# Cutting the first load of a cosine-similarity kernel by partitions: 16 rows, then 112, both issued ahead of the opening barrier

## The chip, the cores and the metric

One core of one Trainium2 chip. The metric is the device time of one execution in microseconds (us); every run below is of state fast with a granted clock of 1.0, except the two benches, which ran once each (state unknown) and are only compared within themselves. "Span" is first to last instruction in the profile, 1.8 to 2.2 us less than the device time here.

## The reference, cut to what matters

```python
x, y: float32 [8192, 8192]
x_norm = np.linalg.norm(x, axis=1, keepdims=True)
y_norm = np.linalg.norm(y, axis=1, keepdims=True)
return np.sum(x * y, axis=1) / (x_norm.squeeze() * y_norm.squeeze() + 1e-8)
```

Both inputs, 537 MB, are read once; for each row three sums are needed.

## The kernel before

The rows come in groups of 256, two rows to a partition, so that one load is 128 partitions x 16384 floats: 64 KB per partition, 8 MiB in all. (Below, a "row" is what one partition takes from one load, 64 KB, and a "row time" is the 2.42 us that it usually needs.) Three slots hold loads, x and y by turns. ScalarE (ACT) squares and sums, VectorE (DVE) forms the dot products, PE's sequencer hands the landings on to both. The last 512 rows come in smaller pieces.

```python
def load(src, m):
    return nc.sync.dma_start(out=slots[m % SLOTS], in_=src).then_inc(landed[m % SLOTS], 16)
...
load(xg[0, 0], 0)
load(yg[0, 0], 1)
load(xg[0, 1], 2)

with nc.sync.Fori(0, R - 1) as r:
    for m in range(SLOTS, 3 * SLOTS):
        ...
        take(nc.sync, used)              # a slot is free again
        load(src[r + g // SLOTS, g % SLOTS], m)
...
with nc.tensor.Fori(0, R):
    for m in range(2 * SLOTS):
        take(nc.tensor, landed[m % SLOTS], 16)
        nc.tensor.sem_inc(for_act, 1)
        nc.tensor.sem_inc(for_dve, 1)
```

A function that runs when the program is finished moves the first DMA instruction ahead of the opening barrier:

```python
load = next(i for i in body.instructions if i.opcode == "DMACopy")
...
opening.instructions = head[:at] + [load] + head[at:]
```

## Time and profile before

| | before |
|---|---|
| device time, median | 1249.38 us (1249.23 to 1249.7, 3 runs) |
| span | 1247.6 us |
| ACT busy / DVE busy | 916.9 / 698.2 us |
| share of 16 DMA engines taken by the load queue | 99.6% |
| first ACTIVATE on data | 22.36 us |

The prediction shows the lines of the profile that carry this. One view more is needed later: what the DMA engines moved in each of 40 equal slices of 31 us, in GB/s, from the page of the kernel before.

```profile
GB/s 435 431 414 435 437 437 437 437 435 435 433 412 437 437 437 437 437 437 435 435 424 420 437 437 437 437 437 437 433 433 412 437 437 437 437 437 437 418 425 335
```

The stream is flat from the first slice to the last but one. The dips I read as the counting of whole 64 KB packets in a slice, for the packets' own times stay at 2.42 us throughout (108 of 7680 took over 2.44).

### The profile page before, as it was taken

Reading aid. Unit: us, or ns where it says so; the run is one execution under the profiler, and the core shown is the slowest. Engines: PE = TensorE matmul, PEld = TensorE weight load, DVE = VectorE, ACT = ScalarE, POOL = GpSimd, SP = SyncE. Lnnn points to the kernel's source line nnn. Section 1 sums busy time; section 2 is a strip of 40 time slices with the busy share of each in tenths; the row PEclk is TensorE's granted clock in tenths of the full one; section 3 lists DMA queues with packets and bytes.
Section 4 is the critical chain, followed back from the end, with each engine's and each line's share of the span. In section 5 each row is a group of like instructions: output and inputs, shape, how many; then the busy total and the mean of one; then the engine's idle time right before and its main releaser. Section 6 shows DMA issues by size and latency. Waiting matters only on the chain. (4 is left out here: it accounts for less than half of the span.)

```text
span 1247.6 us, 1785 instructions
## 1 busy us (share of the span) xinstructions
PE 1.3 (0%) x4; PEld 0.3 (0%) x4; DVE 698.2 (56%) x252; ACT 916.9 (73%) x285; POOL 0.8 (0%) x8
## 2 busy tenths in 40 slices
PE   0000000000000000000000000000000000000000
PEld 0000000000000000000000000000000000000000
DVE  1654576545765447654467544675446755457566
ACT  3686776867768668677686776867868668677888
POOL 0000000000000000000000000000000000000000
DMA  9999999999999999999999999999999999999998
GB/s 435 431 414 435 437 437 437 437 435 435 433 412 437 437 437 437 437 437 435 435 424 420 437 437 437 437 437 437 433 433 412 437 437 437 437 437 437 418 425 335
DMA packets 11575, 536.93 MB, mean 430 GB/s; under 512 B 1299, under 2 KB 1845, under 8 KB 2613
## 3 DMA queue, kind: packets, MB, share of 16 engines
q1 hardware_dynamic: 11528, 536.88, 99.6%
q10 hardware_dynamic: 45, 0.03, 0.0%
q14 instruction: 2, 0.02, 0.0%
HBM read 536.87 MB, written 0.03 MB: 430 GB/s over the span
## 5 line engine op out<-in xcount | busy, mean ns | idle before, releaser
L142 ACT ACTIVATE junk<-slot 128x8192 uint8<-128x8192 f32 (+4 forms) x138 | 900.8, 6528 | 326.2 <-ACTq L139 320.5
L145 DVE CUSTOM_DVE_ANT_0 slot<-slot,slot 128x4096 f32<-128x4096 f32 (+1 forms) x60 | 391.1, 6556 | 452.4 <-DVEq L139 452.4
L212 DVE COPY side<-slot 128x4096 f32<-128x4096 f32 x30 | 132.8, 4428 | 71.7 <-DVEq L139 71.7
L145 DVE CUSTOM_DVE_ANT_0 side<-side,slot,part 128x4096 f32<-128x4096 f32 x30 | 134.6, 4488 | 0.0
L145 DVE CUSTOM_DVE_ANT_0 slot<-slot 128x8192 f32<-128x8192 f32 (+3 forms) x5 | 29.6, 5944 | 20.4 <-ACT junk L142 12.7
L142 ACT ACTIVATION_READ_ACCUMULATOR junk<-slot (+1 forms) x138 | 25.7, 186 | 0.0
L145 DVE CUSTOM_DVE_ANT_0 vjunk<-slot 128x384 uint8<-128x384 f32 (+4 forms) x8 | 6.8, 886 | 1.0 <-DMA slot<-in_y_dram 1.0
L145 DVE DVE_READ_ACCUMULATOR2_ANT gsum<- x60 | 6.7, 112 | 0.0
L145 DVE DVE_READ_ACCUMULATOR2_ANT part<- 128x1 f32 x30 | 2.5, 83 | 0.0
L192 ACT ACT_TABLE_LOAD x1 | 1.3, 1283 | 1.0 <-SPq L168 1.0
L350 PE MATMUL side<-ident,gden 128*30 128x128 f32 x2 | 0.6, 395 | 1196.9 <-DVE gden L344 1196.9
L194 ACT ACT_TABLE_LOAD x1 | 1.3, 1283 | 0.1
L145 DVE DVE_READ_ACCUMULATOR2_ANT parts<- 128x1 f32 x11 | 0.9, 82 | 0.0
L353 DVE COPY orow<-side 30x128 f32<-30x128 f32 x2 | 0.5, 279 | 0.6 <-PE side L350 0.6
L371 ACT COPY dots<-side 4x128 f32<-4x128 f32 x1 | 0.3, 254 | 0.7 <-PE side L369 0.7
L145 DVE CUSTOM_DVE_ANT_0 vjunk<-slot,base 128x384 uint8<-128x384 f32 x1 | 0.6, 619 | 0.1
L381 DVE TENSOR_TENSOR orl<-side,dots 4x128 f32<-4x128 f32 x1 | 0.3, 279 | 0.5 <-PE side L379 0.5
L270 DVE RECIPROCAL gden<-gden 128x60 f32<-128x60 f32 x1 | 0.5, 529 | 0.0
L350 PEld LDWEIGHTS side<-ident,gden 128*30 128x30 f32 x2 | 0.1, 107 | 1196.8 <-issue 1196.8
L369 PE MATMUL side<-ident,bsum 128*4 128x128 f32 x1 | 0.4, 373 | 46.9 <-DVE bsum L145 46.9
L379 PE MATMUL side<-ident,bden 128*4 128x128 f32 x1 | 0.4, 374 | 0.0
L340 ACT ACTIVATE gnorm<-gsum 128x120 f32<-128x120 f32 x1 | 0.3, 302 | 0.0
(25 smaller groups left out, 4.4 us busy)
## 6 DMA issues: line engine op xcount, KB each, us to landing
slot<-in_x_dram SPq DMA_DIRECT2D x3, 4096.0 KB, 29.9
slot<-in_y_dram SPq DMA_DIRECT2D x2, 4096.0 KB, 32.2
slot<-in_y_dram SPq DMA_DIRECT2D x1, 2368.0 KB, 35.8
slot<-in_x_dram SPq DMA_DIRECT2D x1, 1984.0 KB, 32.3
slot<-in_y_dram SPq DMA_DIRECT2D x1, 1728.0 KB, 39.4
slot<-in_y_dram SPq DMA_DIRECT2D x1, 1600.0 KB, 35.7
slot<-in_x_dram SPq DMA_DIRECT2D x1, 1088.0 KB, 37.9
slot<-in_y_dram SPq DMA_DIRECT2D x1, 640.0 KB, 40.2
```

The lines of the kernel that those rows point to most:

```text
L142: return nc.scalar.activation(out=into, in_=src, func=ACTF.Square, accum_out=acc)
L145: return nc.vector.tensor_tensor_reduce(out=into, in0=a, in1=b, scale=1.0, scalar=init, op0=ALU.mult, op1=ALU.add, accum_out=acc)
L192: nc.scalar.memzero(dummy).then_inc(squared, 1)
L194: nc.scalar.sqrt(out=dummy, in_=dummy).then_inc(squared, 1)
L212: nc.vector.tensor_copy(out=side, in_=xt[:, CUT:])
L270: return dve.done(nc.vector.reciprocal(out=den, in_=den))
L340: m_norm = act.done(nc.scalar.activation(out=gnorm, in_=flat(gsum)[:, 0:2], func=ACTF.Sqrt))
L350: mk = pe.done(nc.tensor.transpose(out=t, in_=gden[:, j:2 * G:2], identity=ident))
L353: rows.append(dve.done(nc.vector.tensor_copy(out=orow[:, :, j], in_=t)))
L369: m_xy = pe.done(nc.tensor.transpose(out=psl[0], in_=bsum[:, XY, :], identity=ident))
L371: m_dots = act.done(nc.scalar.copy(out=dots, in_=psl[0]))
L379: mk = pe.done(nc.tensor.transpose(out=psl[1], in_=bden, identity=ident))
```

## The change

The intent: a transfer of 16 partitions is issued first so that data starts to move sooner; the other 112 follow, also ahead of the barrier. No byte more is moved.

```diff
-    load = next(i for i in body.instructions if i.opcode == "DMACopy")
-    assert not load.sync_info.on_wait
+    loads = [i for i in body.instructions if i.opcode == "DMACopy"][:2]
+    assert not any(i.sync_info.on_wait for i in loads)
...
-    opening.instructions = head[:at] + [load] + head[at:]
+    opening.instructions = head[:at] + loads + head[at:]
...
+    HEAD = 16
...
+    first = sem("first")
...
-        load(xg[0, 0], 0)
+        nc.sync.dma_start(out=slots[0][0:HEAD], in_=xg[0, 0, 0:HEAD]).then_inc(first, 16)
+        nc.sync.dma_start(out=slots[0][HEAD:], in_=xg[0, 0, HEAD:]).then_inc(landed[0], 16)
...
+        nc.tensor.wait_ge(first, 16)
         with nc.tensor.Fori(0, R):
```

More of the change, by code (lines that the diff above doesn't have):

```diff
@@ L25, in first_load_and_last_wait @@
     at = 1 + next(n for n, i in enumerate(head)
-                  if i.opcode == "ISA" and i.engine == load.engine)
-    body.instructions = [i for i in body.instructions if i.name != load.name]
-    opening.instructions = head[:at] + [load] + head[at:]
+                  if i.opcode == "ISA" and i.engine == loads[0].engine)
+    body.instructions = [i for i in body.instructions if i.name not in {k.name for k in loads}]
+    opening.instructions = head[:at] + loads + head[at:]
     closing = blocks[-1]
```

## The prediction

The sum came to +15 us: -0.3 for the issue, +7.3 for the 16 rows and 8 (from a span of 7 to 9) for the 112. The grounds of the two larger terms rested on which rows are in flight together and which partitions then slow each other, and nothing that had been run showed it. Of the rivals, A means no loss, B a loss in the 16 rows alone, C one in both parts as in the sum, with only the rows that meet losing time, and D a loss in every row of both.

> **What bounds the kernel now.** I read the page first: busy shares, the slices, the DMA queues. Then the timeline of the first 60 us, then the windows by stage, then the waits, and last the packet records.
>
> The page, parts 1 to 3:
>
> ```profile
> PE 1.3 (0%) x4; PEld 0.3 (0%) x4; DVE 698.2 (56%) x252; ACT 916.9 (73%) x285; POOL 0.8 (0%) x8
> ...
> DMA  9999999999999999999999999999999999999998
> ...
> q1 hardware_dynamic: 11528, 536.88, 99.6%
> ```
>
> No compute engine is near full, while the 16 DMA engines work in every slice, and one queue holds 99.6% of their time. The windows (columns: stretch, length, engines, clock, DMA share, GB/s) say that this is so from the first window on:
>
> ```profile
> 0.00:22.40 22.40, 0.00 (x0) 0.00 (x0) 0.00 (x0) 3.01 (x5) 0.80 (x8) 1.00 1.00 421
> 61.00:1200.00 1139.00, 0.58 (x2) 0.14 (x2) 646.54 (x211) 846.75 (x238) 0.00 (x0) 1.00 1.00 433
> ```
>
> The timeline of the start:
>
> ```profile
> 0.00 0.41 SPq L150 DMA_DIRECT2D slot<-in_x_dram  x1
> ...
> 1.07 0.33 SPq L150 DMA_DIRECT2D slot<-in_y_dram  x1
> ...
> 1.46 0.52 SPq L150 DMA_DIRECT2D slot<-in_x_dram  x1
> ...
> 22.36 7.03 ACT L142 ACTIVATE junk<-slot 128x8192 uint8<-128x8192 f32 x1 [18.25 <-ACTq L139]
> ...
> 41.73 7.03 ACT L142 ACTIVATE junk<-slot 128x8192 uint8<-128x8192 f32 x1 [4.93 <-ACTq L139]
> ...
> 55.31 0.35 SPq L150 DMA_DIRECT2D slot<-in_y_dram  x1
> ...
> 59.99 0.34 SPq L150 DMA_DIRECT2D slot<-in_x_dram  x1
> ```
>
> Three loads of 8 MiB are in the queue by 2 us. The first lands at about 22.3, the second 19.4 later, and a load is issued at 55.31, while the third (landing at 61.0, where ACT starts again) still runs: the queue has 5.7 us of work left at the refill. So compute hides, and the stream of rows sets the end. The waits say the same of ACT and DVE: they wait for landings, never the reverse.
>
> ```profile
> DVE slot L145 <- DVEq L139: 452.4, 30, 15.1
> ACT junk L142 <- ACTq L139: 320.5, 121, 18.2
> ```
>
> The packet records give the unit of account. A packet is one 64 KB partition row, and takes 2.42 us from the second on (16 x 65536 B / 2.42 us = 433 GB/s). Lined up end to start they form 16 lanes; in a lane each row starts within some ns of the end of the one before, and a lane's gaps over the whole run come to under 0.6 us (4 us in one, the final store). So an engine takes one row at a time, has 8 per load and 512 in all: 512 x 2.42 = 1239.0. First packet at 1.04 us, last of the 16 lanes at 1.98; last packets of the inputs near 1241.5 to 1242.6. **Nothing can be caught up: what an engine loses at the start is missing at the end.**
>
> [...]64 KB at a steady 2.42 us in all 16 lanes is 27.1 GB/s per engine with no sign of collisions (108 of the 7680 packets of 64 KB took over 2.44, and two thirds of their excess lies in the first 20 us).
> [...]Here the first packet comes 1.04 us after the start of the issue; the measurement decides.
>
> **The change part by part.**
> *Issue.* The intent must be an earlier first row[...]. The issue instruction took 0.41 us for 128 rows, the first packet came at 1.04 and the last lane began at 1.98. If short issues brought all lanes to 1.04 or a little before, the late lane gains 0.9 at most and the others 0 to 0.4; about 0.3 on what the end waits for. Credit: -0.3, at best -0.9.
> *Second issue before the barrier.* SP reaches the barrier about 0.3 to 0.4 us later, the other engines start later by that, and the y load is issued near 1.5 in place of 1.07. Its first row is needed near 20. ACT's two table loads end at 4.1 and its data comes at 22. Cost: 0.
> *New wait.* PE's sequencer waits once for the 16 rows before its loop. The 112 queue behind them on the same engines, so the loop's first wait ends later anyway. PE does nothing else until 1196. Cost: 0.
> *The 16 rows.* Sixteen engines write partitions 0 to 15 at once.[...]
> *The 112 rows.* [...]
> *After.* y is a 128-partition load[...]. The late engine runs on late to the end. The early ones run ahead until a slot is missing; the refill needs the slowest engine's landing plus some 13.9 us (41.4 to 55.3), against 19.4 per load, so engines may be 5.5 us apart before the leaders stop. That costs the leaders only.
> *Sum:* -0.3 + 7.3 + 8 = +15. The first ACTIVATE would move from 22.4 to about 37, and 1249.4 to 1264.
>
> **The rivals.**
> A. *Harmless split.* [...]Then only the issue part is left: 1248.5 to 1249.5. For it: this trace has no partial-partition load, and both parts together are the same rows on the same 16 engines. [...]I give it 22%.
> B. *Head only.* [...]+7 to +10, 1256 to 1259. For it: the first row of before takes 3.0 to 3.4 us and the second 2.42[...]. Against: packets within a lane never overlap by more than a few ns. 20%.
> C. [...]as in my sum: +13 to +18. 48%.
> D. *Round robin,* [...]in all +58 (1307, over 4%). For it: nothing in the trace. 7%. Other surprises 3%.
> E. *A new wait in compute,* such as the barrier or PE's wait taking the place of DMA. Against: 18 us of slack at the start, and 5 us idle per load in ACT after. It makes nothing of the time.
>
> **Range and chances.** C gives 1262 to 1267, B 1256 to 1259, A 1249. The point is 1264; the range has to hold A, B and C: 1248.5 to 1269. The 2% limits lie at 25 us: 1224.4 cannot be had from a change that touches 2 us of idle queue; 1274.4 needs D or something worse than C. Faster 0.5%, within 2% 91.5%, slower 8%.
>
> **What would show each step right or wrong.** [...]the first 16 packets take near 9.7 us each in place of 3.0 to 3.4; at 3 us A holds. Deal of the 112: packets between 10 and 37 us have times of 2.42 and about 4.84 mixed (C), all 2.42 (B), or all near 9.7 (D). The first ACTIVATE's start tells the sum: 22 (A), 30 (B), 37 (C), 80 (D). After the y load all rows are back at 2.42 and the shift stays constant to the end; if the end shifts less than the first landing, some of the stream's loss is made up, and my "nothing can be caught up" is wrong. Issue: first packet earlier than 1.04 and the last lane earlier than 1.98, else the credit is 0. The prediction fails as a whole if the late part is compute: ACT or DVE idle less than the 5 us per load of before.

## The result, and the profile after

The changed kernel took 1270.34 us in the median (1269.96 to 1270.59, 6 runs), beside 1249.41 for the kernel before in the same rounds: **+20.9 us**. The ratio is 1.0166, interval 1.0153 to 1.0179. (A ratio here is the mean time of one kernel's runs over that of the other's of the same rounds, so not quite the ratio of the medians.) This is well clear of noise, and 1.3 us outside the predicted range.

The timeline of the start after the change (columns: start, duration, engine, line, operation, operands; in brackets the idle time before it and what ended it):

```profile
0.00 0.41 SPq L172 DMA_DIRECT2D slot<-in_x_dram  x1
...
0.46 0.40 SPq L173 DMA_DIRECT2D slot<-in_x_dram  x1
...
1.52 0.35 SPq L152 DMA_DIRECT2D slot<-in_y_dram  x1
...
43.87 7.03 ACT L144 ACTIVATE junk<-slot 128x8192 uint8<-128x8192 f32 x1 [39.30 <-ACTq L141]
...
63.25 7.03 ACT L144 ACTIVATE junk<-slot 128x8192 uint8<-128x8192 f32 x1 [4.94 <-ACTq L141]
...
76.83 0.35 SPq L152 DMA_DIRECT2D slot<-in_y_dram  x1
```

The first landing, as ACT sees it, moved from 22.36 to 43.87, by 21.5 us. From there on nothing changed: the second follows 19.4 us later, as before (19.37), ACT again idles 4.9 us before it, and the refill comes 13.6 us after that landing (55.31 - 41.73 before, 76.83 - 63.25 after). All of the loss lies in the first load, and nearly all of it is still there at the end: +20.9 us by the medians, +20.4 by the spans of the two profiled runs (1268.0 - 1247.6). The DMA and GB/s lines of the page:

```profile
DMA  9999999999999999999999999999999999999998
GB/s 223 368 430 430 430 430 434 430 434 442 438 434 430 430 430 432 432 430 438 444 436 430 430 430 430 434 430 434 440 440 434 430 430 430 430 434 430 430 430 332
```

Only the first two slices of the GB/s are low. The busy share does not show the loss: the DMA line is the same in both kernels. The windows of the changed kernel (stretch, length, DVE, ACT and the other engines' busy times, clock, DMA share, GB/s):

```profile
1.00:10.40 9.40, 0.00 (x0) 0.00 (x0) 0.00 (x0) 2.97 (x4) 0.59 (x4) 1.00 1.45 216
10.40:42.00 31.60, 0.00 (x0) 0.00 (x0) 0.00 (x0) 0.00 (x0) 0.00 (x0) 1.00 0.90 230
42.00:61.00 19.00, 0.00 (x0) 0.00 (x0) 4.43 (x1) 14.24 (x4) 0.00 (x0) 1.00 1.02 442
```

The engines are taken 0.9 of the time while they move 230 GB/s, half the usual rate (442 in the last window). (The first window counts whole packets that only began in it, hence a share above 1.) The waits name no new culprit; only the wait for the first landing grew, from 18.2 to 39.3 us for ACT and from 22.5 to 44.0 for DVE:

```profile
DVE slot L147 <- DVEq L141: 452.4, 30, 15.1
ACT junk L144 <- ACTq L141: 341.2, 121, 39.3
DVE side L216 <- DVEq L141: 92.8, 30, 44.0
```

What happened inside shows in the packet records. I took the 64 KB packets in order of start, 16 to a group (the n-th row of every lane), and sorted the 16 durations of a group in us:

```
after           starts         durations of the 16 rows
row 1 (the 16)   1.03.. 1.72   8.02 8.08 8.18 ... 9.12 9.21 9.43
row 2 (112)      9.16..10.57   5.01 5.10 5.15 ... 5.62 5.69 5.83
row 3           14.85..15.57   4.64 4.64 4.64 ... 4.67 4.71 4.85
row 4           19.49..20.21   2.85 2.85 2.90 ... 3.14 | 4.70 4.73
row 5           22.63..24.81   3.55 3.65 3.68 ... 3.69 | 4.39 4.47
row 6           26.32..28.36   4.20 4.24 4.26 ... 4.65 4.66 4.73
row 7           30.51..32.90   4.57 4.57 4.57 ... 4.72 4.73 4.83
row 8           35.08..37.62   4.48 4.48 4.49 ... 4.75 4.79 4.82
row 9 (y)       39.58..42.43   2.66 2.70 2.77 ... 3.15 3.33 3.37
row 10          42.94..45.29   2.42 2.42 2.42 ... 2.42 2.43 2.43
before: row 1   2.48 to 3.42, rows 2 to 11 all 2.42; row 10 starts 23.39..23.99
```

The 16 rows take 8.0 to 9.4 us, three to four times 2.42, as predicted. But in five of the seven rows of the 112 **all sixteen** packets need about twice 2.42 (4.2 to 5.8), and only in rows 4 and 5 are there two slow ones (4.4 to 4.7) and fourteen faster (2.85 to 3.69). The first packet starts no sooner (1.03 against 1.04); the last of the first sixteen starts at 1.72 against 1.98.

### The profile page after: what moved, and what is told of

It is laid out like the page before. It is cut to its first block, busy times and chain, and to the rows that moved or that the text cites. A ratio compares the mean times of both kernels' runs of the same rounds, so it can differ in the third digit from the quotient of the medians.

```text
span 1268.0 us, 1786 instructions
## 1 busy us (share of the span) xinstructions
PE 1.3 (0%) x4; PEld 0.3 (0%) x4; DVE 698.2 (55%) x252; ACT 916.9 (72%) x285; POOL 0.8 (0%) x8
```

## The experiments

Theories. **P**: it is the destination; rows that are written at the same time into certain partitions of SBUF slow each other. (Below they "clash"; the texts say "share" or "meet". Which partitions clash I had assumed.) **Local sharing**: P, and only the rows that clash lose time. **C**: P, and in addition a clash slows rows that have no part in it. **H**: it is the source, the addresses in HBM. **K**: counts that are no power of two are slow. **S**: it is the start, that is a small transfer at the head, a second issue ahead of the barrier, or the new wait.

### 1. A bench of single loads (probe1)

A program that only loads, one transfer at a time; a small memset on DVE marks each landing, and the next load is issued after it. Its output is zeros, so wrong.

```diff
+ one(b[0:16], xs[1, 0:16])            # 16 rows, as in the change
+ one(a[16:128], xs[2, 16:128])        # the 112
+ one(a[16:128], xs[4, 0:112])         # the 112, source from another row
+ one(b[:, 0:2048], xs[11, 0:16].rearrange("p (a f) -> (p a) f", a=8))  # the 16 rows' bytes over 128 partitions
+ ... and 32, 48, 64, 80, 96, 128 partitions, 16 and 32 at a step of 8 and 4, 112 and 128 rows of 16 KB
```

> A bench of single loads, one at a time, each waited for before the next is issued; its output is zeros on purpose. Theory P[...]: 16 partitions take 9.7 us of transfer, as long as four rows one after the other, wherever the 1 MiB comes from, and the same 1 MiB dealt over 128 partitions takes 2.4 to 3. 64 partitions take 19.4, as long as 128 do. 16 partitions at a step of 8 partitions[...]: 4.8. [...]In the changed kernel the 112 took about 30 after the 16[...]. Rival H (the source side: the addresses read from HBM, not the destination, are what is slow): the same 1 MiB into 128 partitions is as slow as into 16, and the 112 change their time when their source starts at another row. Rival K (a count of rows that is no power of two is slow to generate or to deal): 112, 96, 80 and 48 are slow, 16, 32 and 64 run at full rate of 2.4 us per 16 rows.

The timeline of the bench; the idle time in brackets is issue to landing as DVE saw it:

```profile
34.98 0.06 DVE L31 MEMSET mark<- 128x1 f32 x1 [11.75 <-DMA slot<-in_x_dram]
68.21 0.06 DVE L31 MEMSET mark<- 128x1 f32 x1 [33.17 <-DMA slot<-in_x_dram]
...
135.00 0.06 DVE L31 MEMSET mark<- 128x1 f32 x1 [33.90 <-DMA slot<-in_x_dram]
...
289.25 0.06 DVE L31 MEMSET mark<- 128x1 f32 x1 [4.88 <-DMA slot<-in_x_dram]
...
370.46 0.06 DVE L31 MEMSET mark<- 128x1 f32 x1 [22.01 <-DMA slot<-in_x_dram]
```

In order: the 16 rows, the 112, the 112 from another source row, 1 MiB of 16 DRAM rows spread over 128 partitions, and a whole load. The same kind of megabyte takes 11.75 us into 16 partitions and 4.88 into 128, and the 112 are as slow from another source: H falls. (The spread megabyte moves in packets of 8 KB, so this comparison alone would leave a doubt. The 16 whole rows into partitions at a step of 8 took 7.64 us, each packet 4.3 to 5.1, near the 4.8 expected; experiment 5 has the cleaner pair.) 64 partitions took 22.93 us, about as long as 128: K falls, though 48, 80, 96 were slow too (26.67, 27.38, 32.03). The two parts add up to the change: a whole load is 22.01 with eight row times of 2.42, so one row time alone would be 22.01 - 7 x 2.42 = 5.07 and seven 19.59; the 16 cost 11.75 - 5.07 = **6.7** and the 112 cost 33.17 - 19.59 = **13.6**, in all 20.3.

The packets of the 112 took 31.5 us, and they show rows of two kinds: a few with two slow packets and fourteen faster ones, and all others with sixteen slow ones:

```
112 from partition 16: rows 3, 4      e.g. row 4: 14 of 3.05 to 3.33, two of 4.42 and 4.81
112 from partition  0: rows 4, 5      e.g. row 5: 14 of 3.17 to 3.40, two of 4.42 and 4.67
all other rows after the first: all sixteen between 3.65 and 4.93
```

With local sharing I had expected mixed rows, some packets at 2.42 and some at twice that; no packet of the 112 is at 2.42, and in most rows all sixteen are slow. That is theory C, formed here and put in its strongest form: any clash slows all 16.

### 2. The cut at 64 (half)

```diff
-    HEAD = 16
+    HEAD = 64
```

> The changed kernel with the cut at 64 in place of 16, so 64 and 64 partitions. P: [...]four rows per engine at half rate, 19.4 us each, so the first load takes 38.7 in place of 19.4 and the end moves by +19, to 1268 to 1269. K (odd counts): 64 is a power of two, no loss, 1249. S (the second issue ahead of the barrier, or the small first transfer, costs): about 1249 to 1250, as the issue is the same two instructions.

1270.77 us against 1249.36, ratio 1.0172 (1.0156 to 1.0187): +21.4. All eight rows of the first load took 4.5 to 5.3, those after the first nearly all 5.12 us, which is 2.12 and not 2.00 times 2.42. A power of two does not help, so K is out. The rows take some 6% more than the half rate expected: six rows at 5.12 and one at 4.93 in place of 4.84 are +1.8 us, and the estimate of +19.4 lacked 2.0.

### 3. The cut along the columns (cols)

```diff
-        nc.sync.dma_start(out=slots[0][0:HEAD], in_=xg[0, 0, 0:HEAD]).then_inc(first, 16)
-        nc.sync.dma_start(out=slots[0][HEAD:], in_=xg[0, 0, HEAD:]).then_inc(landed[0], 16)
+        nc.sync.dma_start(out=slots[0][:, 0:HEAD], in_=xg[0, 0, :, 0:HEAD]).then_inc(first, 16)
+        nc.sync.dma_start(out=slots[0][:, HEAD:], in_=xg[0, 0, :, HEAD:]).then_inc(landed[0], 16)
-    HEAD = 16
+    HEAD = 2048
```

> The split along the columns: first 128 partitions of 2048 elements, 1 MiB as in the change, then the rest of the 128 partitions; both ahead of the barrier and the new wait kept. P: no loss[...]: 1249.0 to 1249.6, the first ACTIVATE again near 22.4 us. S (two transfers, the second issue ahead of the barrier or the new wait cost the 21 us): 1260 to 1270.

1249.72 against 1249.36, ratio 1.0002 (0.9988 to 1.0016): no difference. Two issues ahead of the barrier, a first transfer of 1 MiB and the new wait are all there, so S falls. The profiled run's first ACTIVATE:

```profile
21.94 7.03 ACT L144 ACTIVATE junk<-slot 128x8192 uint8<-128x8192 f32 x1 [17.35 <-ACTq L141]
```

It comes 0.4 us sooner than the 22.36 of before, but the end does not.

### 4. Another load, late in the run (late)

The kernel before, with the x half of the first of the last four tiles (32 KB per partition) cut at 16 (not shown: that piece's semaphore now counts to 32):

```diff
-                nc.sync.dma_start(out=p.src, in_=p.dram).then_inc(p.mark[0], 16)
+                if p.mark[1] == 32:
+                    nc.sync.dma_start(out=p.src[0:16], in_=p.dram[0:16]).then_inc(p.mark[0], 16)
+                    nc.sync.dma_start(out=p.src[16:], in_=p.dram[16:]).then_inc(p.mark[0], 16)
+                else:
+                    nc.sync.dma_start(out=p.src, in_=p.dram).then_inc(p.mark[0], 16)
```

> The kernel before, with the first load untouched, and another load cut at 16 partitions: the x half of the first of the last four tiles, 128 x 8192, half as many bytes per row, late in the run. P, with nothing to be caught up: half the loss of the change, +10.5 us, 1259 to 1261. S (a matter of the start: barrier, first issue, cold HBM): 1249 to 1250. If the queue's slack near the end absorbs it: +0 to +5.

1260.07 against 1249.36: +10.7, half of the change's loss for half its bytes (ratio 1.0087, 1.0071 to 1.0102). The place makes no difference here, and the queue, full as it is at that point, absorbs nothing. The dip sits where the load is, in the third slice from the end:

```profile
GB/s 433 433 433 432 433 433 433 433 433 433 433 433 433 436 433 433 433 431 436 433 433 433 433 433 433 433 433 433 433 433 433 433 433 433 433 433 416 284 430 338
```

### 5. A bench of windows of 64 partitions (probe2)

A window of 64 partitions starts at 32, 28, 24, 20, 16, 8, 0: a scale of doses. In the first bench the window at 0 was slow (22.93 us); at 32 I expected no clash at all, and the further the start from 32, the more.

```diff
+ one(b[32:96], xs[1, 32:96]);  one(a[28:92], ...);  one(b[24:88], ...);  one(a[20:84], ...)
+ one(b[16:80], ...);  one(a[8:72], ...);  one(b[0:64], ...)
+ one(a[8:120], ...);  one(b[4:116], ...)
+ one(a[0:128:2], xs[10, 0:64]);  one(b[1:128:2], ...);  ...
```

> A second bench of single loads, zeros as output on purpose. The first bench showed that 112 partitions run at about 1.93 row times per row[...], and at 1.26 to 1.5 with two rows left at 1.9[...]. Theory C[...]: a window of 64 partitions that starts at 32, 28, 24, 20, 16, 8, 0[...]. At 32 all rows take 1.0 row times (2.42 us), 4 MiB in about 10 us; at 28 most rows 1.2 to 1.5; from 24 on all 16 rows near 1.9 to 2.1, so that 24 costs as much as 0: about 20 us. Local sharing, as I predicted: at 24 four rows of 16 take 2 and twelve take 1[...]; the landing is 20 us at all but 32. [...]112 partitions from 8 on: step 4[...] should fall to about 1, with all others near 1.9[...]. Every second partition (64 at a step of 2): [...]the bench found 32 at a step of 4 without any sharing[...], so 1.0 would not surprise me.

```profile
35.35 0.06 DVE L31 MEMSET mark<- 128x1 f32 x1 [12.46 <-DMA slot<-in_x_dram]
57.19 0.06 DVE L31 MEMSET mark<- 128x1 f32 x1 [21.79 <-DMA slot<-in_x_dram]
79.63 0.06 DVE L31 MEMSET mark<- 128x1 f32 x1 [22.38 <-DMA slot<-in_x_dram]
...
171.06 0.06 DVE L31 MEMSET mark<- 128x1 f32 x1 [22.92 <-DMA slot<-in_x_dram]
...
249.15 0.06 DVE L31 MEMSET mark<- 128x1 f32 x1 [12.48 <-DMA slot<-in_x_dram]
```

These are the windows at 32, 28, 24 and 0, and the even partitions. The rows, in units of 2.42 us, sorted (second row of each transfer):

```
window at 32:                     1.00 x16
window at 28:                     1.00 x14, 2.06 2.07
window at 24:                     2.10 x16
windows at 20, 16, 8, 0:          2.10 to 2.12, all 16
112 from 8, row 4:                1.05 to 1.28; its rows 2, 3, 5, 6, 7: 1.75 to 2.07
even partitions, 64 at a step of 2: 1.00 x16
```

This decides between local sharing and C. Four partitions away from 32 only two rows lose, as local sharing has it; a second such window, at 36, gave the same (14 rows of 1.00, two of 2.11). Eight away, local sharing had four slow rows of sixteen, which is also the two of the window at 28 doubled (estimate); all sixteen are slow, at 2.10, and they get no slower with a start further off (2.10 to 2.12). C as it was put, in which any clash slows all 16, fails here: my expectation had "1.2 to 1.5" for the window at 28; it was 1.00. From here on C means: one pair of slow rows stays alone (windows at 28 and 36), and from the window at 24 on all 16 are slow. And the even partitions show no clash (1.00 x16). Their expectation was open. They also settle H: the even partitions and the window at 0 take rows 0 to 63 of a tile as their source, and need 12.48 and 22.92 us.

### 6. Two whole loads ahead of the barrier (two_ahead)

```diff
-        nc.sync.dma_start(out=slots[0][0:HEAD], in_=xg[0, 0, 0:HEAD]).then_inc(first, 16)
-        nc.sync.dma_start(out=slots[0][HEAD:], in_=xg[0, 0, HEAD:]).then_inc(landed[0], 16)
+        load(xg[0, 0], 0)
...
-        nc.tensor.wait_ge(first, 16)
```

> The kernel before with its first two loads, x and y, uncut, both issued ahead of the opening barrier: the part of the change that moves a second issue ahead of the barrier, alone. [...]nothing is lost or gained, 1249.0 to 1249.6. Rival (the later barrier delays what the end depends on): +0.4 to +20.

1249.37 against 1249.40, ratio 0.9998 (0.9984 to 1.0012): the second issue ahead of the barrier is worth nothing and costs nothing.

### 7. Three parts, with the window at 32 (mid)

```diff
-        nc.sync.dma_start(out=slots[0][0:HEAD], ...)
-        nc.sync.dma_start(out=slots[0][HEAD:], ...)
+        nc.sync.dma_start(out=slots[0][32:96], in_=xg[0, 0, 32:96]).then_inc(first, 16)
+        nc.sync.dma_start(out=slots[0][0:32], in_=xg[0, 0, 0:32]).then_inc(first, 16)
+        nc.sync.dma_start(out=slots[0][96:128], in_=xg[0, 0, 96:128]).then_inc(landed[0], 16)
-        nc.tensor.wait_ge(first, 16)
+        nc.tensor.wait_ge(first, 32)
```

> The first load of x cut into three: partitions 32 to 95, then 0 to 31, then 96 to 127. [...]the first part[...] four row times; the other two[...] four row times each: 12 in all against 8, +4 x 2.42 = +9.7, about 1259 to 1260. If any cut of the partitions costs the same: 1270. If 64 partitions[...] share at all cuts: +19 to +21.

1260.62 against 1249.40: +11.2 (ratio 1.0089, 1.0073 to 1.0104), 0.6 to 1.6 above the expected 1259 to 1260. Rows 2 to 4 took 2.42, rows 5 to 8 from 4.4 to 5.1. With 2.11 in place of 2 (fitted after the run, from the benches) the estimate is (4 + 4 x 2.11 - 8) x 2.42 = +10.7.

### 8. Even and odd partitions (evenodd)

```diff
-        nc.sync.dma_start(out=slots[0][0:HEAD], ...)
-        nc.sync.dma_start(out=slots[0][HEAD:], ...)
+        nc.sync.dma_start(out=slots[0][0:128:2], in_=xg[0, 0, 0:128:2]).then_inc(first, 16)
+        nc.sync.dma_start(out=slots[0][1:128:2], in_=xg[0, 0, 1:128:2]).then_inc(landed[0], 16)
```

(The +19 to +21.5 on record is for the case that the halves clash as at the cut at 64; why they might is cut.)

> The first load of x cut into even and odd partitions, 64 each. [...]+19 to +21.5, 1268 to 1271. If the deal of such a transfer avoids sharing, as 32 at a step of 4 did in the first bench: no loss, 1249 to 1250.

1249.74 against 1249.40, ratio 1.0003 (0.9988 to 1.0019). A cut of the partitions need not cost anything: after the first, all rows took 2.42, so none clashed; again 64 and 64, but +0.3 in place of +21.4.

### 9. Two new cuts as a test of the rule (head80, head112)

```diff
-    HEAD = 16
+    HEAD = 80      # the other run: 112
```

The rule is C, with the row times of the benches.

> The changed kernel with the cut at 80, a test of the rule on a cut that no run has had[...]. 80 partitions from 0: five steps[...], 5 x 2.05 = 10.3 row times; 48 from 80: three steps[...], 3 x 3.38 = 10.1; 20.4 against 8, so +12.4 x 2.42 = +30 us, about 1279 to 1280, over 2% slower.[...]

> The changed kernel with the cut at 112: the large transfer first, then the 16. By the same rule and the bench (112 from partition 0 took 31.2 us of transfer with the start, 16 took 9.5): 12.6 + 3.9 = 16.5 row times against 8, +20.6 us, about 1270, the same as the change: the order of the two does not matter, and the first packet's earlier start has no part in it. If the loss came from a small transfer standing at the head of the queue: under +5.

head80: 1279.80 against 1249.41, ratio 1.0242 (1.0225 to 1.026), +30.4 us where the row times of the benches had +30. (The expectation takes them from the first bench, which had 80 and 48 partitions from 0; new are the 48 from 80, and that the parts add up in the kernel.) Rows 2 to 5 took 4.86 to 5.17, row 7 from 8.04 to 8.46. head112: 1270.38 (ratio 1.0167, 1.015 to 1.0184), +21.0 where the benches had +20.6: the order of the parts does not matter. Timeline of head80:

```profile
52.72 7.03 ACT L144 ACTIVATE junk<-slot 128x8192 uint8<-128x8192 f32 x1 [48.15 <-ACTq L141]
```

### What stays open

Why one pair of slow rows stays alone (windows at 28 and 36) and all sixteen are slow from the window at 24 on is not known: the traces show neither what lies between a DMA engine and SBUF nor the engine of a packet. So which partitions are in flight together, and which of them clash, is not shown either, only which transfers were slow: 16, 32, 48, 80, 96 and 112 contiguous partitions from every start tried (from 11.51 us for 16 to 33.90 for 112, issue to landing), and 64 from every start but 32 (all rows 1.00) and, but for two rows of sixteen, 28 and 36. 128 partitions, and 64 at a step of 2 (12.48 us), showed no clash; 32 at a step of 4 took 8.13 us beside 12.44 for 32 contiguous ones. Nor is the loss in proportion to the row everywhere: with rows of 16 KB the 112 took 8.55 us in the first bench beside 7.15 for 128. Worked as above, with a row time of 0.6, that is 2.0 us lost, where a quarter of the 13.6 would be 3.4. This was not followed up.

## Why the prediction was right or wrong

- **What bounds the kernel:** right. The stream of rows does; the end kept 20.4 to 20.9 of the 21.5 us by which the first landing moved, and the late cut cost its full half.
- **Issue, -0.3:** wrong by that little. The first packet started at 1.03 instead of 1.04. The last lane began at 1.72 instead of 1.98, but at 1.68 in two_ahead and 1.54 in late, whose first loads are whole, so this is scatter and not the short issue; and no run with an early cut was faster. An issue of 16 rows took 0.41 us like one of 128, and one of 64 took 0.58 (half).
- **Second issue before the barrier, new wait:** right at 0, by the runs cols and two_ahead.
- **The 16 rows, +7.3:** right in size. The bench gives +6.7.
- **The 112 rows, +7 to 9:** this is the step that failed. What was wrong is the assumption that only the rows that clash lose time. In five of the seven rows all sixteen packets took 4.2 to 5.8 us. The bench gives +13.6 for this term. The window at 24 shows the wrong step by itself: all sixteen rows at 2.10.
- **The sum, +15 and 1262 to 1267 for C, range to 1269:** too low by the missing 5 to 6 us of that term, so the measured 1270.34 lies outside. I had no trace of a clash and trusted a sharing rule that I made up; the range should have held the case in which a clash holds up all sixteen: with every row of the 112 at twice 2.42, 7 x 2.42 = +16.9 in place of 8, and +24 in all with the sum's other terms (estimate).
- **Rivals:** A (harmless) and D (round robin, +58) fall. B (the 16 rows alone, +7 to +10) falls too. E is right: compute made nothing of it.
- **Signs named ahead:** first packets near 9.7 (8.0 to 9.4 seen, with the rest showing as a long row 2), mixed 2.42 and 4.84 (84 of the 112 between 4.2 and 5.8, the other 28 between 2.85 and 3.69: neither C nor B as I wrote them), first ACTIVATE at 37 (43.87).

## What to carry to other kernels

On a kernel whose DMA engines never rest, an inefficient transfer cost its excess at the end (shown for the first load, +20.9 of 21.5 us, and for one about 90 us before the end, +10.7), and the busy share did not show it (the same DMA line before and after): look at GB/s per slice and at the packets' own durations. When a load has to be cut, cut it along the free dimension (cols, +0.4) or take every second partition (evenodd, +0.3); partitions 32 to 95 ran freely too (all rows 1.00), but with the two parts that then remain mid cost 11.2 us; a contiguous cut at 16, 64, 80 or 112 cost 21 to 30 us on 8 MiB. No cut gained anything. And when rows may clash, put into the range the case that a clash holds up all, as it did here from the window at 24 on.
